# Attention slots in another order: score products, exponentials, transposes and products with v regrouped, projection further ahead

## The chip, the cores and the metric

One core of one Trainium2 chip runs the whole program in one launch. The metric is the device time of one execution, in microseconds (us). An engine here is one of five in-order instruction streams: PE (TensorE, matmuls and transposes), DVE (VectorE), ACT (ScalarE), POOL (GpSimd) and SP (SyncE, which issues most of the DMA transfers).

## The reference, cut to what matters

The program is a trunk of two layers on a sequence of 1024 positions with 1024 features. The first layer mixes positions by a gated MLP; the second by attention; each is followed by a squared-ReLU MLP with 4096 hidden features, and a layer norm closes every part. The change touches the attention of the second layer alone:

```python
def dilated_branch(q, k, v, window, dilation, slopes):
    # blocks of span = window // dilation = 128 positions, each with the block before it
    s = jnp.einsum('bnqrhe,bnkrhe->bnrhqk', qb, kb) * (E ** -0.5)
    s = jnp.where(valid, s + bias, NEG)
    m = jnp.max(s, axis=-1, keepdims=True)
    p = jnp.exp(s - m)
    l = jnp.sum(p, axis=-1, keepdims=True)
    o = jnp.einsum('bnrhqk,bnkrhe->bnqrhe', p / l, vb)
    return o, m + jnp.log(l)

def mixer_b(h, w_qkv, w_out, slopes):
    qkv = (h @ w_qkv).reshape(B, S, 3, 3, 16, 64)
    # three patterns (window, dilation): (128, 1), (512, 4), (2048, 16)
    # each through dilated_branch; the outputs are merged by a softmax over their lse
    return o.reshape(B, S, 1024) @ w_out
```

All of it is float32. A product of two float32 matrices is made of three matmuls: each operand is split into a high part and a low part (`hi`, `lo`), and hi*hi, hi*lo and lo*hi are summed.

## The kernel before

The work of attention is cut by pairs of heads (`hp`, eight of them) and by patterns (`g`, in the order 2, 1, 0; pattern 0 is dilation 1). That makes 24 units, and `attend(n, ...)` (L1367) plans one of them. Each of the 24 units owns eight slots, from `base = 8 * n` on, and reaches over into the slots of the units behind it. A slot has two halves. `at(slot, pos)` (L1362) appends a function to the list of a half slot; at the end (L1774 and following) the halves are gone through in order, the functions of each are called in the order in which they were appended, and behind each half some steps of the projection follow. One step of the projection (`project`, L1323) is three matmuls of 512 columns that add to a sum of q or k (`psq`, `psk`). Steps are dealt out by a credit: 48 of them (`lead = 6 * KD`) come ahead of the first slot, and each half slot earns 464/351 of a step. So PE alternates between small work of the slots and steps of the projection, which fill the time in which the slots wait for ACT and DVE.

The functions of one unit are these:

- `scores(m)` (L1411), for each group of two to four tiles of 128 queries, at the first half of a slot in `starts`: the matmuls `sc` for both heads into two PSUM banks, then for each tile and head a reduction on DVE (L1445: scale, bias, minimum, into `p` and `stat`) and an exponential on ACT (L1447, with a sum). A group has four to eight such pairs.
- `transposes(m)` (L1473), at the second half of a slot: two to four transposes of `p` on PE into a bank `pT`, then the split of that bank: the high part `pThi` on ACT (L102) and the low part `pTlo` on DVE (L103).
- `weighted(m)` (L1486), three half slots later: the products `pv` of `pThi` and `pTlo` with v, into two banks for each head. With the last pack of a head the banks are copied and added into `oT` (L1508 on ACT, L1509 on DVE).
- `merge(hp, ...)` (L1539) joins the three patterns of a pair of heads: statistics go through DRAM (`st_dram`, `mst`), the factors come back as `bc`, and twelve half products (`scale` L1593, `add` L1597, `cut`) on DVE follow, from 16 half slots behind its base on.

The projection splits a sum into `qhi`/`qlo` or `khi`/`klo` (L102, L103), which the scores of patterns 2 and 1 read. Its weights are loaded and split by `unit` (`wq_hi`, `wq_lo`, `wk_hi`, `wk_lo`); the load and the split of a weight are both asked for one unit ahead of its use. Pattern 0 has its q and k from DRAM (`bq`, `bk`).

Toward the end, the output projection begins while attention still runs (`begin`, L1744, matmuls `psoa`, `psob`), with weights that `staged_unit` (L1672) loads, multiplies by a gate (L1682) and splits (`wo_hi`, `wo_lo`). The scheduler that builds the program keeps most of the order in which functions are called, and moves instructions where it takes their inputs to be late.

PSUM banks in attention: two each for `sc`, `pv`, `pT` (kind `tr`) and the projection (kind `mm`).

## Time and profile before

| | us |
|---|---|
| median of three runs | 2759.44 (2755.86 to 2762.37) |
| profiled execution, its own time | 2759.17 |
| its span, first to last instruction | 2757.5 |
| first projection matmul of attention | 1378.7 |
| first score matmul | 1411.6 |
| last reduction of attention | 2042.6 |

The span is shorter than the execution's own time by what lies around the program. In rows of the profile, a line such as L1447 is the place in the kernel's text, a name such as `pv<-pThi,v` tells what is written and what is read, and a bracket behind a row tells how long the engine was idle ahead of it and what it waited for. A row of a stretch has: the stretch, its length, the busy time of PE, PEld (weight loads of PE), DVE, ACT and POOL with counts, the granted share of PE's clock, the share of the DMA engines, and GB/s.

### The profile page before, as it was taken

The numbers are of one execution on the slowest core, as the hardware profiler recorded it, in microseconds if no ns is written. First come the engines' busy times: TensorE is split into PE (matmuls) and PEld (weight loads), VectorE is DVE, ScalarE is ACT, GpSimd is POOL, SyncE is SP. The second block draws the span as 40 slices with busy tenths as digits, with TensorE's granted clock in tenths as the row PEclk, the third lists the DMA queues.
The fourth block names the chain that finished last, engine by engine and source line by source line (L and its number), as shares of the span: only waits on it lengthen the run. The fifth ranks groups of instructions, "written<-read, shape, count | busy, mean of one in ns | idle before, by whom it ended". The sixth has DMA issues, their size and how long they took to land. (4 is left out here: it accounts for less than half of the span.)

```text
span 2757.5 us, 36894 instructions
## 1 busy us (share of the span) xinstructions
PE 2678.4 (97%) x13242; PEld 2206.1 (80%) x13242; DVE 1991.9 (72%) x3594; ACT 1375.1 (50%) x2593; POOL 96.3 (3%) x161
## 2 busy tenths in 40 slices
PE   6999999999999999999999999999999999999998
PEld 5788888887888878888887887778777788878886
DVE  6787698787877788555556676666668966568877
ACT  3354475555443464343445665555564755544432
POOL 1000000000000001111110000000010000000000
PEclk9999999999999999999999999999999999999999
DMA  7534347667836546555556455444573554485562
GB/s 260 161 120 133 115 142 230 217 222 262 317 130 198 177 152 216 194 201 195 182 176 176 120 140 141 110 120 136 169 197 122 185 204 142 153 305 195 175 205 86
DMA packets 332572, 487.98 MB, mean 177 GB/s; under 512 B 50988, under 2 KB 176340, under 8 KB 332388
## 3 DMA queue, kind: packets, MB, share of 16 engines
q1 hardware_dynamic: 318564, 435.29, 49.8%
q0 software_dynamic: 13824, 50.34, 5.1%
q8 instruction: 104, 1.70, 0.3%
q14 instruction: 80, 0.66, 0.1%
HBM read 357.01 MB, written 128.53 MB: 176 GB/s over the span
## 5 line engine op out<-in xcount | busy, mean ns | idle before, releaser
L796 PE MATMUL psua<-right,left 128*128 128x512 f32 x1536 | 364.8, 391 | 0.3
L955 PE MATMUL psd<-rhi,lhi 128*128 128x512 f32 x896 | 350.4, 391 | 3.0 <-ACT part L827 3.0
L955 PE MATMUL psd<-rlo,lhi 128*128 128x512 f32 x896 | 350.3, 391 | 0.2
L955 PE MATMUL psd<-rhi,llo 128*128 128x512 f32 x896 | 349.8, 390 | 0.0
L796 PEld LDWEIGHTS psua<-right,left 128*128 128x128 f32 x1536 | 288.2, 189 | 62.1 <-DVE right L103 1.3
L1447 ACT ACTIVATE p<-p,stat 128x128 f32<-128x128 f32 (+1 forms) x384 | 168.1, 439 | 112.0 <-DVE stat L1445 112.0
L955 PEld LDWEIGHTS psd<-rhi,lhi 128*128 128x128 f32 x896 | 169.1, 189 | 39.3 <-ACT part L827 3.9
L955 PEld LDWEIGHTS psd<-rhi,llo 128*128 128x128 f32 x896 | 169.1, 189 | 35.4
L955 PEld LDWEIGHTS psd<-rlo,lhi 128*128 128x128 f32 x896 | 168.8, 188 | 35.6 <-DVE rlo L103 1.1
L796 PE MATMUL psuc<-right,left 128*128 128x512 f32 x768 | 187.2, 390 | 0.0
L103 DVE TENSOR_TENSOR pTlo<-pT,pThi 128x512 fp32r<-128x512 f32 (+1 forms) x160 | 99.1, 621 | 110.3 <-ACT pThi L102 109.8
L796 PEld LDWEIGHTS psuc<-right,left 128*128 128x128 f32 x768 | 143.5, 188 | 30.0 <-DVE right L103 0.4
L128 DVE SCALAR_TENSOR_TENSOR adaacc<-adaw,silu_c,adaacc 128x512 f32<-128x512 f32 x168 | 128.4, 774 | 54.0 <-DMA adaw<-in_ada_w_dram 53.5
L103 DVE TENSOR_TENSOR left<-ws,left 128x512 fp32r<-128x512 f32 x128 | 87.7, 687 | 72.0 <-ACT left L102 70.2
L103 DVE TENSOR_TENSOR llo<-lraw,lhi 128x1024 fp32r<-128x1024 f32 x112 | 136.3, 1217 | 0.8 <-ACT lhi L102 0.8
L1345 PE MATMUL psq<-form_L,wq_hi 128*128 128x512 f32 x384 | 130.7, 422 | 0.0
L1345 PE MATMUL psk<-form_L,wk_hi 128*128 128x512 f32 x384 | 130.3, 418 | 0.0
L102 ACT CAST left<-ws 128x512 fp32r<-128x512 f32 x128 | 79.1, 620 | 100.3 <-DVE ws L717 87.6
L1257 PE MATMUL psv<-vrhi,form_S 128*128 128x512 f32 x384 | 119.8, 390 | 1.2 <-DVE vpart L1223 0.7
L102 ACT CAST rhi<-rraw 128x1024 fp32r<-128x1024 f32 x48 | 50.6, 1053 | 139.6 <-issue 113.8
L102 ACT CAST lhi<-lraw 128x1024 fp32r<-128x1024 f32 x112 | 117.4, 1048 | 3.4 <-PE psua L796 2.9
L1445 DVE CUSTOM_DVE_ANT_0 p<-sc,bias 128x128 f32<-128x128 f32 (+1 forms) x384 | 110.0, 345 | 7.6 <-PE sc L1431 5.1
(326 smaller groups left out, 6117.7 us busy)
## 6 DMA issues: line engine op xcount, KB each, us to landing
lraw<-forms SPq DMA_DIRECT2D x112, 512.0 KB
adaw<-in_ada_w_dram SPq DMA_DIRECT2D x192, 256.0 KB
up<-in_mlp_w_up_dram SPq DMA_DIRECT2D x64, 512.0 KB
forms<-s SPq DMA_DIRECT2D x128, 256.0 KB
rraw<-in_mlp_w_down_dram SPq DMA_DIRECT2D x64, 512.0 KB
forms<-part SPq DMA_DIRECT2D x96, 256.0 KB
v<-vs POOLq DMA_DIRECT2D x48, 512.0 KB, 3.7
vraw<-in_b_w_qkv_dram SPq DMA_DIRECT2D x42, 512.0 KB
```

Of the source, the lines that this page charges most:

```text
L102: first = A.copy(hi, src) if hi_engine is A else hi_engine.tensor_copy(hi, src)
L103: return first, lo_engine.tensor_tensor(lo, src, hi, op=ALU.subtract)
L128: ins = V.scalar_tensor_tensor(acc[:], raw[:], silu_c[:, k : k + 1], acc[:], ALU.mult, ALU.add)
L796: T.matmul(acc, w[:, a, k, :], right[p][:, b, k, :], start=p in (1, 2, 5) and k + a + b == 0, stop=k == 3 and a == 1, skip_group_check=True)
L955: ins = T.matmul(sums[kind, m][:], l[a][:, k, m * P : (m + 1) * P], r[b][:, k, :], start=p in (1, 5, 2, 3) and kp + k + a + b == 0, stop=k ...
L1257: T.matmul(acc, rows[:, m * P : (m + 1) * P], cols_, start=p in (1, 2, 5) and kp + k + a + b == 0, stop=kp == 1 and k == 1 and a == 1, ski ...
L1345: T.matmul(p[:], wu[a][:, k * P : (k + 1) * P], h_op(k, half, b), start=k + c_ == 0, stop=k == KD - 1 and c_ == 2)
L1445: V.tensor_tensor_reduce(out=pr, in0=banks[e][:, sl], in1=st["bias"][:, width - w :], scale=-0.125, scalar=3e38, op0=ALU.add, op1=ALU.min, ...
L1447: A.activation(pr, pr, AF.Exp, bias=nm, scale=-1.0, accum_out=l)
```

## The change

Each function now goes into its half slot with a rank, and the functions of a half slot are called by rank: transposes and products with v first (0), then score matmuls (1), then the split of the transposed probabilities and the copies out of the `pv` banks (2), then reductions and exponentials (3), then all else (4). The reductions and exponentials of a group leave `scores` and become `soften(m, part)`: the first half of the tiles in the half slot of the scores, the rest in the next half slot. The transposes stand one half slot earlier, and with them the products with v, still three half slots behind. The copies out of the banks (`gather`) come one half slot behind the last product. The merge's twelve pieces start one slot later. The projection's lead is 56 steps instead of 48, and 456/351 of a step follows each half slot. A weight of the projection is loaded three units ahead and split one unit ahead.

```diff
@@ project
-                units = {key: load(*key) for key in todo[:2]}
+                raw, units = {}, {}
+                def load(i):
+                    if i < len(todo):
...
+                        t = raw[i] = wts.tile([P, D], F32, name=f"w{'qk'[X]}_{hp}_{g}_raw", tag="raw", bufs=2)
+                        nc.sync.dma_start(...)
+                def cut(i):
+                    if i < len(todo):
+                        units[todo[i]] = tuple(wts.tile([P, D], F32R, name=f"wqk_{i}_{m}", tag=f"w{m}")[:] for m in ("hi", "lo"))
+                        split(*units[todo[i]], raw.pop(i)[:])
+                for i in range(2):
+                    load(i)
+                cut(0)
+                load(2)
...
                     if half == 1:
-                        if 1 <= i < len(todo) - 1:
-                            units[todo[i + 1]] = load(*todo[i + 1])
+                        cut(i + 1)
+                        load(i + 3)
@@ at
-            def at(slot, pos):
+            def at(slot, pos, rank=4):
                 def put(f):
-                    slots[slot][pos].append(f)
+                    slots[slot][pos].append((rank, f))
                 return put
+            def in_half(half_slot, rank):
+                return at(half_slot // 2, half_slot % 2, rank)
@@ attend
-                    for t, w, sl in spans:
+                    my["spans", m] = banks, spans
+                def soften(m, part):
+                    stat = my["stat"]
+                    banks, spans = my["spans", m]
+                    cut = (len(spans) + 1) // 2
+                    for t, w, sl in spans[cut:] if part else spans[:cut]:
...
-                    at(base + slot, 0)(lambda m=m: scores(m))
+                    at(base + slot, 0, 1)(lambda m=m: scores(m))
+                    for part in range(2):
+                        at(base + slot, part, 3)(lambda m=m, part=part: soften(m, part))
...
+                        pT[m] = pst, end
+                    def halve(m, h=h, pT=pT):
+                        pst, end = pT[m]
                         hi = work.tile([P, HALF], F32R, name=f"pThi_{h}_{g}_{m}", tag="h")
...
-                        if m < len(packs) - 1:
-                            return
+                    def gather(e=e, rows=rows, pvs=pvs):
                         oT = oT_of(e)
...
-                            half_slot = 2 * (base + 5 + 4 * e + w) + 1
+                            half_slot = 2 * (base + 5 + 4 * e + w)
                             then = half_slot + 3
-                        at(half_slot // 2, half_slot % 2)(lambda m=m, f=transposes: f(m))
-                        at(then // 2, then % 2)(lambda m=m, f=weighted: f(m))
+                        in_half(half_slot, 0)(lambda m=m, f=transposes: f(m))
+                        in_half(half_slot, 2)(lambda m=m, f=halve: f(m))
+                        in_half(then, 0)(lambda m=m, f=weighted: f(m))
+                    in_half(then + (not last_one), 2)(gather)
@@ merge
-                    n = pace * n + 16
+                    n = pace * n + 18
@@ the loop over the slots
-            lead, credit = 6 * KD, 0
+            lead, credit = 7 * KD, 0
...
-                    for f in pos:
+                    for _, f in sorted(pos, key=lambda x_: x_[0]):
                         f()
```

What this makes of the order shows at three places. The first is ACT in the fourth pair of heads, where the second group of pattern 2 (`p_6_2`, `p_7_2`) has its exponentials, while the pair before still transposes (`pThi_5_0_3` is the high part of head 5, pattern 0, pack 3). Before:

```order
L1447 ACTIVATE p_6_2_4_14420,stat_3_2_14209<-p_6_2_4_14420,stat_3_2_14209 128x128
L1447 ACTIVATE p_7_2_4_14423,stat_3_2_14209<-p_7_2_4_14423,stat_3_2_14209 128x128
L1447 ACTIVATE p_6_2_4_14420,stat_3_2_14209<-p_6_2_4_14420,stat_3_2_14209 128x128
L1447 ACTIVATE p_7_2_4_14423,stat_3_2_14209<-p_7_2_4_14423,stat_3_2_14209 128x128
L1447 ACTIVATE p_6_2_6_14430,stat_3_2_14209<-p_6_2_6_14430,stat_3_2_14209 128x128
L1447 ACTIVATE p_7_2_6_14433,stat_3_2_14209<-p_7_2_6_14433,stat_3_2_14209 128x128
L1447 ACTIVATE p_6_2_6_14430,stat_3_2_14209<-p_6_2_6_14430,stat_3_2_14209 128x128
L1447 ACTIVATE p_7_2_6_14433,stat_3_2_14209<-p_7_2_6_14433,stat_3_2_14209 128x128
L102 COPY pThi_5_0_3_14451<-pT_5_0_3_14447 128x384
```

On the same engine at the same place now:

```order
L102 COPY pThi_5_0_3_14425<-pT_5_0_3_14395 128x384
L1469 ACTIVATE p_6_2_4_14429,stat_3_2_14243<-p_6_2_4_14429,stat_3_2_14243 128x128
L1469 ACTIVATE p_7_2_4_14432,stat_3_2_14243<-p_7_2_4_14432,stat_3_2_14243 128x128
L1469 ACTIVATE p_6_2_4_14429,stat_3_2_14243<-p_6_2_4_14429,stat_3_2_14243 128x128
L1469 ACTIVATE p_7_2_4_14432,stat_3_2_14243<-p_7_2_4_14432,stat_3_2_14243 128x128
L1469 ACTIVATE p_6_2_6_14465,stat_3_2_14243<-p_6_2_6_14465,stat_3_2_14243 128x128
```

The high part has moved from behind the eight exponentials to ahead of them. The second place is DVE a little later, ahead of the first group of pattern 1 (`p_6_1_0`), whose scores read `klo_3_1`. Before:

```order
L103 TENSOR_TENSOR pTlo_6_2_0_14497<-pT_6_2_0_14491,pThi_6_2_0_14496 128x512
L1593 TENSOR_TENSOR bc_2_2_14458<-oT_2_2_13674,bc_2_2_14458 128x512
L103 TENSOR_TENSOR wk_4_1_lo_14981<-wk_4_1_raw_14978,wk_4_1_hi_14980 128x1024
L103 TENSOR_TENSOR klo_3_1_14283<-psk_3_1_0_14440,khi_3_1_14282 128x4x128
L1509 TENSOR_TENSOR oT_3_2_14616<-oT_3_2_14616,pv_6_2_0_14524 64x512
L1445 ISA p_6_1_0_14559,stat_3_1_14534<-sc_6_1_0_14539,bias_6_1_14535 128x128
```

DVE at the same place now:

```order
L103 TENSOR_TENSOR klo_3_1_14222<-psk_3_1_0_14358,khi_3_1_14221 128x4x128
L103 TENSOR_TENSOR wqk_19_lo_14927<-wk_4_1_raw_14496,wqk_19_hi_14926 128x1024
L1537 TENSOR_TENSOR oT_2_0_14349<-oT_2_0_14349,pv_5_0_1_14363 64x512
L103 TENSOR_TENSOR pTlo_6_2_0_14521<-pT_6_2_0_14511,pThi_6_2_0_14520 128x512
L1537 TENSOR_TENSOR oT_3_2_14653<-oT_3_2_14653,pv_6_2_0_14536 64x512
L103 TENSOR_TENSOR pTlo_6_2_1_14580<-pT_6_2_1_14549,pThi_6_2_1_14579 128x512
L1467 ISA p_6_1_0_14583,stat_3_1_14554<-sc_6_1_0_14559,bias_6_1_14555 128x128
```

The low part of k has moved ahead of the weight's low part, and the merge's product (`bc_2_2`) has left this place. The third place is DVE in the last pair of heads, where the weights of the output projection are prepared (`wo_0` to `wo_3`) and the merge of the pair before runs (`bc_6`). Before, these rows stood ahead of the reductions of the first group of pattern 1 (`p_14_1_0`), with the low parts of `wo_0` and `wo_1` a few rows ahead of them:

```order
L1682 TENSOR_TENSOR wo_2_raw_18254<-wo_2_raw_18254,gate_2_18126 128x1024
L1682 TENSOR_TENSOR wo_3_raw_18291<-wo_3_raw_18291,gate_2_18126 128x1024
L103 TENSOR_TENSOR wo_2_lo_18297<-wo_2_raw_18254,wo_2_hi_18296 128x1024
L1593 TENSOR_TENSOR bc_6_2_18236<-oT_6_2_17449,bc_6_2_18236 128x512
L1445 ISA p_14_1_0_18353,stat_7_1_18328<-sc_14_1_0_18333,bias_14_1_18329 128x128
```

DVE there now, from the reductions of the next group (`p_15_1_3`) on:

```order
L1467 ISA p_15_1_3_18457,stat_7_1_18332<-sc_15_1_1_18432,bias_15_1_18335 128x256
L1467 ISA stat_7_1_18332 128x1
L1712 TENSOR_TENSOR wo_2_raw_18254<-wo_2_raw_18254,gate_2_18135 128x1024
L103 TENSOR_TENSOR wo_1_lo_18288<-wo_1_raw_18137,wo_1_hi_18287 128x1024
L1623 TENSOR_TENSOR bc_6_1_18237<-oT_6_1_17766,bc_6_1_18237 128x512
L103 TENSOR_TENSOR wo_2_lo_18297<-wo_2_raw_18254,wo_2_hi_18296 128x1024
L1467 ISA p_14_1_5_18461,stat_7_1_18332<-sc_14_1_1_18431,bias_14_1_18333 128x256
```

The low parts of `wo_1` and `wo_2` have moved from ahead of the reductions of the first group of pattern 1 into those of the second.

8 lines of the change are left out of this document (4 added, 4 removed).

## The prediction

> **What bounds the kernel now.** I read the page's busy times first, then the busy times of two stretches, then who waited for whom in the first of them, and last the instructions in order of time around two of those waits.
>
> ```profile
> span 2757.5 us, 36894 instructions
> PE 2678.4 (97%) x13242; PEld 2206.1 (80%) x13242; DVE 1991.9 (72%) x3594; ACT 1375.1 (50%) x2593; POOL 96.3 (3%) x161
> 1412.00:1978.00 566.00, 547.86 (x3570) 454.39 (x3568) 379.06 (x1154) 334.99 (x1010) 20.57 (x48) 0.98 0.49 132
> 1978.00:2080.00 102.00, 94.02 (x553) 76.71 (x551) 74.68 (x184) 56.87 (x146) 10.07 (x12) 0.95 0.76 200
> ```
>
> PE is busy for 97% of the span, so only PE's idle time, the overlap it loses around a wait, and its clock can be won. The change touches attention alone. Its even part runs from 1412 to 1978 us: there PE is idle for 566.0 - 547.9 = 18.1 us and has 0.98 of its clock, while DVE (379 of 566) and ACT (335 of 566) have room. Everything ahead of 1412 and behind 2080 us stays as it is, bound by PE.
>
> The waits of PE, and then those of its weight loads, in that stretch (total, times, longest):
>
> ```profile
> PE pv L1499 <- ACT pThi L102: 8.9, 12, 1.7
> PE sc L1431 <- DVE klo L103: 6.1, 4, 2.1
> PE pv L1499 <- DVE pTlo L103: 2.0, 8, 0.4
> PEld pv L1499 <- ACT pThi L102: 16.8, 18, 2.1
> PEld pv L1499 <- DVE pTlo L103: 9.3, 25, 0.5
> PEld sc L1431 <- DVE klo L103: 6.7, 4, 2.2
> ```
>
> Two things are late. One is the high and low part of the transposed probabilities, which the products with v (pv) need. This is one such place:
>
> ```profile
> 1657.03 0.27 PE L1476 MATMUL pT<-ident,p 128*128 128x128 f32 x1
> 1657.95 0.40 ACT L1447 ACTIVATE p<-p,stat 128x128 f32<-128x128 f32 x1 [1.69 <-DVE stat L1445]
> 1659.01 0.62 PE L1345 MATMUL psk<-form_L,wk_hi 128*128 128x512 f32 x2
> 1659.70 0.62 PE L1345 MATMUL psk<-form_L,wk_hi 128*128 128x512 f32 x2
> 1661.05 0.46 ACT L102 CAST pThi<-pT 128x384 fp32r<-128x384 f32 x1
> 1661.56 0.38 PE L1499 MATMUL pv<-pThi,v 128*128 128x256 f32 x1 [1.00 <-ACT pThi L102]
> 1662.15 0.38 PE L1499 MATMUL pv<-pTlo,v 128*128 128x256 f32 x1 [0.21 <-DVE pTlo L103]
> ```
>
> The last transpose is done at 1657.3. Its high part starts only at 1661.05, since ACT runs the eight exponentials of a group first, from 1657.95 on. PE reaches the products at about 1660.6 and stands.
>
> The other late thing is the low part of k, without which the scores of the next group cannot go on:
>
> ```profile
> 1666.79 1.05 DVE L1593 TENSOR_TENSOR bc<-oT,bc 128x512 f32<-128x512 f32 x1 [1.50 <-DMA bc<-w_dram]
> 1667.77 1.21 DVE L103 TENSOR_TENSOR wk_lo<-wk_raw,wk_hi 128x1024 fp32r<-128x1024 f32 x1
> 1668.90 0.68 DVE L103 TENSOR_TENSOR klo<-psk,khi 128x512 fp32r<-128x512 f32 x1
> 1669.63 0.33 PE L1431 MATMUL sc<-klo,qhi 64*128 64x128 f32 x2 [1.86 <-DVE klo L103]
> ```
>
> DVE first waits 1.50 us for a transfer that a merge needs, then does the merge's product and a weight's low part, and klo last. PE pays 1.86 us. Four stretches around such waits show what follows (the third column from the end is the granted clock):
>
> ```profile
> 1666.00:1676.00 10.00, 8.14 (x48) 6.84 (x48) 6.00 (x18) 3.80 (x14) 0.00 (x0) 0.83 0.71 189
> 1741.00:1751.00 10.00, 8.29 (x37) 6.30 (x35) 4.94 (x10) 5.31 (x18) 0.81 (x2) 0.83 0.87 215
> 1830.00:1840.00 10.00, 7.96 (x48) 6.54 (x46) 6.75 (x19) 3.80 (x14) 0.00 (x0) 0.83 0.71 183
> 1909.00:1921.00 12.00, 9.94 (x50) 8.30 (x49) 6.71 (x19) 5.19 (x16) 0.00 (x0) 0.72 0.62 167
> ```
>
> PE works slower for some us after each.
>
> **The change, part by part.** Nothing is computed more or less often: the rows on each engine are the same in kind and number, only their places move. So every price is a wait that goes or comes.
>
> *Parts ahead of exponentials (ranks, two halves, transposes half a slot earlier).* On ACT the high part now stands ahead of the group's exponentials, and at most the second half of the group before, four exponentials, stands ahead of it. From the transposes to their products it is still three half slots. The loss today: PE idle 8.9 + 2.0 = 10.9 us, and each of the 18 + 25 = 43 waits of a load also loses the overlap of two matmuls. Three projection matmuls take 1659.70 - 1659.01 = 0.69 us, so one starts each 0.23 us, while a pair shows 0.62 and thus a single one 0.39: 0.16 us lost per wait, 43 x 0.16 = 6.9 us. Together 17.8 us. I take 15.3 of it, since a weight's high part (1.05 us on ACT) or a copy still gets between now and then; the bounds are 9 and 17.8.
>
> *k in time (eight more projection steps ahead, the merge a slot later, ranks).* The lead grows from 48 to 56 steps, that is 8 x 0.69 = 5.5 us of PE work moved ahead of the first scores. It costs nothing, as the same work is missing later: 464/351 steps per half slot become 456/351, and both streams end at half slot 351. At the wait shown (slot 80 of 175) about 4 of the 8 steps of lead are left, and on DVE klo now stands ahead of the weight's part and the merge's product. A stall of 2 us is covered by either. PE's 6.1 us are worth 4 x 0.16 more: 6.7, and I take 6.2, bounds 5 and 6.7; the last pairs keep little of the lead.
>
> *The clock.* The four stretches lose 3 x 10 x 0.17 + 12 x 0.28 = 8.5 us. Each follows directly on an idle time of PE of 1.7 to 2.1 us. With those waits gone I count all of it back: 8.5, bounds 0 and 8.5. Yet of two equal waits the second brought a drop and the first did not:
>
> ```profile
> 1516.18 0.33 PE L1499 MATMUL pv<-pThi,v 128*128 128x128 f32 x1 [1.69 <-ACT pThi L102]
> 1743.45 0.39 PE L1499 MATMUL pv<-pThi,v 128*128 128x256 f32 x1 [1.71 <-ACT pThi L102]
> 1514.00:1524.00 10.00, 8.08 (x48) 6.12 (x46) 6.29 (x17) 5.85 (x20) 0.00 (x0) 1.00 0.15 43
> ```
>
> So the link is not one to one. [...]
>
> *Products and the copies out of them (gather) later.* The copies of a head's sums come half a slot later than its last product. The next head's first product needs the first bank only, and the order still has that bank's copy ahead of the head's last parts. Price zero; without that cover each of the 48 heads would wait for a copy and an addition:
>
> ```profile
> L102 ACT CAST wq_hi<-wq_raw 128x1024 fp32r<-128x1024 f32 x13 | 13.7, 1055 | 5.2 <-PE psq L1345 5.1
> L1447 ACT ACTIVATE p<-p,stat 128x128 f32<-128x128 f32 (+1 forms) x344 | 150.2, 438 | 103.6 <-DVE stat L1445 103.5
> L1508 ACT COPY oT<-pv 64x512 f32<-64x512 f32 x82 | 47.6, 581 | 60.4 <-PE pv L1499 59.3
> L103 DVE TENSOR_TENSOR pTlo<-pT,pThi 128x512 fp32r<-128x512 f32 (+1 forms) x138 | 85.5, 621 | 95.8 <-ACT pThi L102 95.4
> L1509 DVE TENSOR_TENSOR oT<-oT,pv 64x512 f32<-64x512 f32 x82 | 56.0, 683 | 24.2 <-ACT oT L1508 22.7
> L1593 DVE TENSOR_TENSOR bc<-oT,bc 128x512 f32<-128x512 f32 x36 | 33.0, 934 | 7.9 <-DMA bc<-w_dram 7.8
> L1445 DVE CUSTOM_DVE_ANT_0 p<-sc,bias 128x128 f32<-128x128 f32 (+1 forms) x344 | 98.0, 343 | 7.3 <-PE sc L1431 4.9 <-issue 1.8
> ```
>
> *Weights loaded two units earlier.* On SP a load now waits until the weight in its buffer has been split, about 2.3 us (1.05 on ACT, 1.22 on DVE). Behind it stand loads of v and of q and k blocks and the merge's small ones, all asked for a slot or more ahead (the first and the third of the four stretches lie 164 us, or two pairs of heads of 24 slots, apart: a slot is 3.4 us). Price zero, and up to 3 us if one of them had no such lead.
>
> *The merge a slot later.* DVE's 7.8 us of waiting for bc go. The four oT buffers come free a slot later, and the next one is asked for eight slots on. Zero.
>
> *The end of attention.* This speaks against the change. From 1985 on PE fills its time with the output projection (psoa), whose weights DVE prepares:
>
> ```profile
> 2004.43 1.22 DVE L103 TENSOR_TENSOR wo_lo<-wo_raw,wo_hi 128x1024 fp32r<-128x1024 f32 x1
> 1986.73 0.39 PE L1499 MATMUL pv<-pThi,v 128*128 128x256 f32 x1 [0.54 <-ACT pThi L102]
> 2005.71 0.50 PE L1726 MATMUL psoa<-wo_lo,oTs 128*128 128x512 f32 x1 [0.18 <-DVE wo_lo L103]
> 1931.45 1.16 PE sc L1431 x18
> 1934.54 0.84 PE pv L1499 x8
> ```
>
> Before, between the reductions of that group (p_14_1_0) and the end of wo_3's low part DVE has six reductions, a pTlo, three merge products and the part itself: 6 x 0.343 + 0.62 + 3 x 0.93 + 1.22 = 6.7 us. Now it has ten reductions, six merge products, two copies' additions, two pTlo, a merge addition (as long as klo's 0.68) and five weight operations ahead of that point: 3.4 + 5.6 + 1.4 + 1.2 + 0.7 + 6.1 = 18.4 us. PE has some 11 us of its own until there (48 score rows at 1.16/18, 31 transposes and products at 0.84/8, 20 psoa at 0.23: 3.1 + 3.3 + 4.6). So it stands for about 8 us, where the eight waits of before between 1985 and 2007, whose first and last are shown, sum to 3.4: 5 us more, and 1 us for the clock. I take +6, bounds 0 and +12 (the whole 11.7 us of delay).
>
> **Sum**, against the profiled execution's own time of 2759.17 us (span 2757.5 and 1.7 around it; the median of the runs is 2759.44, 0.3 away): 15.3 + 6.2 + 8.5 = 30.0 won, 6 lost, so 2759.2 - 24.0 = 2735.2. **I predict 2735 us.**
>
> **Rivals.**
> [...]
> - *The parts stay late.* ACT's high parts still come behind a second half of exponentials, 4 x (0.44 + a readout) on ACT and a weight's part; then half of 17.8 comes back and part of the clock is not won: 2735 + 6.4 + 6 = 2747 to 2753. Against: three half slots are 5.1 us, and ACT is busy for 335 of 566.
> - *The end takes it back.* DVE becomes the bound there (74.7 busy of 102 us already), the delay of 11.7 us falls on PE in full, and the clock is halved twice as long: 12 + 3.4 + a late chain of transfers behind it, 2745 to 2759.
> - *Slower: the banks of the products.* Each head's sums are copied half a slot later. If the copy of the first bank comes behind the next head's parts, PE stands at 48 changes of head for a copy and an addition, 0.58 + 0.68 = 1.27 us, 61 us in all; with 24 won, 2796. It decides from the point where the first bank's copy starts less than 1.3 us ahead of the next head's first product; half of the heads at that price already give 2765. For it: the copies stand behind the parts now. Against: the order keeps the first bank's copy two packs ahead.
> - That the scheduler sorts the rows back is ruled out by the rows in the section on the change.
>
> **How the numbers follow.** Chances: forecast 0.56, clock stays 0.10, parts late 0.12, end takes it back 0.10, banks 0.12. The low end is all three gains at their upper bounds and a tail that costs nothing, 2759 - 33 = 2726, less some 6 us of waits in the tail (3.4 and clock) that might go too: 2720. The high end is the lower bounds, 9 + 5 + 0, against a loss of 12: 2757. The range 2720 to 2757 takes in all but the banks, and a little of the end's case. A measurement of this kernel can tell about 0.2%, 5.5 us, from no change. Faster by more: 0.56 + 0.10 + 0.09 + 0.04 = 0.79. Within: 0.03 + 0.05 = 0.08. Slower: 0.01 + 0.12 = 0.13.
>
> **What would show it.** In the changed profile, in the stretch that answers to 1412 to 1978: PE's waits for pThi and pTlo fall from 10.9 us to about 2, those for klo from 6.1 to under 1, the granted clock is 1.00, and the stretch is some 30 us shorter. In the end, PE waits more for wo parts and pTlo, DVE in front of it. Waits of pv for DVE's or ACT's oT would mean the banks. The prediction is wrong if pT begins to wait for the exponentials, since transposes come half a slot earlier and second halves half a slot later, or if the stretch is free of waits and yet no shorter.

## The result and the profile after

| | before | changed |
|---|---|---|
| median of the runs, us | 2760.03 (2755.86 to 2762.37, 4 runs) | 2727.61 (2725.15 to 2728.55, 4 runs) |
| profiled execution, its own time | 2759.17 | 2727.96 |
| first to last projection matmul | 611.9 (1378.9 to 1990.7) | 579.4 (1377.0 to 1956.4) |
| from there to the last psoa or psoe | 134.8 (to 2125.6) | 139.0 (to 2095.4) |

The change made the kernel faster: the ratio is 0.9883, 95% interval 0.9866 to 0.9900. In the profiled executions 31.2 us went. The stretch of the projection gave 32.5, the end of attention took 4.2 back, and 3.0 came from outside attention (1.9 ahead, 1.1 behind). Those 3.0 are probably not the change's: before has stretches at half clock (granted share 0.50) of 3.41 us each at 424 and 2441 us that this profile lacks, and another execution with the changed order (no_lead, below) has one at 423 us again.

In the code after, the lines that matter have moved: L1345 is L1358 (projection), L1431 is L1447 (`sc`), L1445 and L1447 are L1467 and L1469 (reductions, exponentials), L1499 is L1527 (`pv`), L1508 and L1509 are L1536 and L1537 (copies into `oT`), L1593 is L1623 (the merge's product `bc`), L1726 is L1756 (`psoa`).

The page of the changed kernel, span and busy times:

```profile
span 2726.2 us, 36911 instructions
PE 2658.8 (98%) x13242; PEld 2196.3 (81%) x13242; DVE 1989.8 (73%) x3594; ACT 1377.1 (51%) x2593; POOL 97.0 (4%) x161
```

The number of instructions on each of these engines is as before. PE's busy time fell from 2678.4 to 2658.8 us with the same instructions: the profile shows matmuls at half clock, and those right behind a wait, as longer (a projection matmul in before 0.63 us at 1672.2, at half clock, and 0.39 us at 1673.9, at full clock again; a `pv` of 128x128 in the changed kernel 0.33 us at 1967.7, behind a wait, and 0.27 to 0.28 us from 1968.7 to 1969.1). Now the projection's stretch and the end of attention, first of before, then of the changed kernel (stretch, length, busy times of PE, PEld, DVE, ACT and POOL, granted clock, DMA share, GB/s):

```profile
1379.00:1991.00 612.00, 593.12 (x3795) 491.46 (x3793) 405.44 (x1209) 352.59 (x1047) 26.23 (x57) 0.99 0.51 141
1991.00:2126.00 135.00, 125.91 (x681) 102.48 (x680) 101.93 (x245) 72.50 (x160) 8.21 (x10) 0.96 0.62 173
```

```profile
1377.00:1957.00 580.00, 576.82 (x3798) 483.94 (x3798) 402.68 (x1208) 353.63 (x1047) 27.09 (x57) 1.00 0.54 149
1957.00:2096.00 139.00, 127.87 (x679) 104.24 (x678) 102.86 (x246) 73.63 (x160) 7.70 (x10) 0.95 0.62 167
```

PE's idle time in the stretch went from 18.9 to 3.2 us, and its clock is whole. DVE and ACT do the same work in less time. PE's waits there in the changed kernel, all that the trace has (total, times, longest):

```profile
PE pv L1527 <- DVE pTlo L103: 2.7, 4, 1.2
PE pv L1527 <- ACT pThi L102: 0.3, 1, 0.3
```

Waits for `klo` are gone, waits for the parts fell from 10.9 us to 3.0. This is the place of the first `order` pair of the change, a pack of three transposes beside the exponentials of the second group:

```profile
1649.52 0.27 PE L1500 MATMUL pT<-ident,p 128*128 128x128 f32 x1
1649.83 0.48 ACT L102 CAST pThi<-pT 128x384 fp32r<-128x384 f32 x1 [0.60 <-PE pT L1500]
1651.65 0.40 ACT L1469 ACTIVATE p<-p,stat 128x128 f32<-128x128 f32 x1 [1.34 <-DVE stat L1467]
...
1654.58 0.29 PE L1527 MATMUL pv<-pThi,v 128*128 128x256 f32 x1
```

The high part starts as soon as the last transpose is done (1649.52 + 0.27; in before 3.75 us behind it), ahead of the exponentials. PE reaches the products 4.3 us later and does not stand. One number went the wrong way, DVE's wait for the merge's factors (the group of all products of the merge, with the idle time ahead of them):

```profile
L1623 DVE TENSOR_TENSOR bc<-oT,bc 128x512 f32<-128x512 f32 x48 | 45.0, 944 | 19.8 <-DMA bc<-w_dram 16.2 <-issue 3.6
```

Before it was 7.8 us, all for `bc`; of the 19.8 us now, 16.2 are for `bc`, and for 3.6 the trace names nothing that was waited for. Most of the experiments turn on it. And in the end of attention, these rows stand around PE's longest wait:

```profile
1963.92 1.98 DVE L1623 TENSOR_TENSOR bc<-oT,bc 128x512 f32<-128x512 f32 x2 [1.97 <-DMA bc<-w_dram]
1965.99 1.07 ACT L1536 COPY oT<-pv 64x512 f32<-64x512 f32 x2 [2.69 <-DVE bc L1623]
1967.08 0.58 ACT L102 CAST pThi<-pT 128x512 fp32r<-128x512 f32 x1
1967.71 0.33 PE L1527 MATMUL pv<-pThi,v 128*128 128x128 f32 x1 [3.26 <-ACT pThi L102]
```

Read from the top: DVE stands for `bc`; the copy out of `pv` needs a buffer of `oT` that this product still reads, so ACT stands; the high part is queued behind the copy; PE stands. No weight of the output projection is in this chain. PE's second longest wait there is another matter:

```profile
1976.36 1.21 DVE L1712 TENSOR_TENSOR wo_raw<-wo_raw,gate 128x1024 f32<-128x1024 f32 x1
1977.50 0.67 DVE L103 TENSOR_TENSOR pTlo<-pT,pThi 128x512 fp32r<-128x512 f32 x1
1978.22 0.33 PE L1527 MATMUL pv<-pTlo,v 128*128 128x128 f32 x1 [2.27 <-DVE pTlo L103]
```

The high part of this pack was done by 1972.5, but DVE had work without a pause from 1966.6 on. From 1969.09 to the low part that is four operations on weights of the output projection (4.8 us), four merge products (3.3 us) and two reductions. This is the queue that the prediction had described.

### The profile page after: what moved, and what is told of

The parts are those of the page before. It is cut to its first block, busy times and chain, and to the rows that moved or that the text cites. A ratio compares the mean times of both kernels' runs of the same rounds, so it can differ in the third digit from the quotient of the medians.

```text
span 2726.2 us, 36911 instructions
## 1 busy us (share of the span) xinstructions
PE 2658.8 (98%) x13242; PEld 2196.3 (81%) x13242; DVE 1989.8 (73%) x3594; ACT 1377.1 (51%) x2593; POOL 97.0 (4%) x161
## 4 chain that ended last, share of the span: by engine, by line
PE 77%; DVE 12%; DMA 6%; ACT 3%; issue 2%; SPq 1%; DVEq 0%; ACTq 0%
PE psd L955 22%; PE psv L1257 13%; PE psua L796 7%; PE psq L1358 6%; PE psk L1358 6%; DMA adaw<-in_ada_w_dram 3%; PE psuc L796 3%; PE psd_wout L389 3%; PE psu L368 3%; PE pv L1527 3%; PE sc L1447 2%; PE psv L470 2%; PE psub L796 2%; DVE adaacc L128 1%; DVE left L103 1%
## 5 line engine op out<-in xcount | busy, mean ns | idle before, releaser
L1469 ACT ACTIVATE p<-p,stat 128x128 f32<-128x128 f32 (+1 forms) x384 | 168.7, 441 | 107.8 <-DVE stat L1467 104.7
L1358 PE MATMUL psk<-form_L,wqk_hi 128*128 128x512 f32 x384 | 127.0, 412 | 0.0
L1358 PE MATMUL psq<-form_L,wqk_hi 128*128 128x512 f32 x384 | 126.4, 410 | 0.0
L1467 DVE CUSTOM_DVE_ANT_0 p<-sc,bias 128x128 f32<-128x128 f32 (+1 forms) x384 | 113.6, 346 | 6.7 <-PE sc L1447 5.8
```

The lines of the kernel that those rows point to most:

```text
L1358: T.matmul(p[:], wu[a][:, k * P : (k + 1) * P], h_op(k, half, b), start=k + c_ == 0, stop=k == KD - 1 and c_ == 2)
L1467: V.tensor_tensor_reduce(out=pr, in0=banks[e][:, sl], in1=st["bias"][:, width - w :], scale=-0.125, scalar=3e38, op0=ALU.add, op1=ALU.min, ...
L1469: A.activation(pr, pr, AF.Exp, bias=nm, scale=-1.0, accum_out=l)
```

## The experiments

Twelve kernels. The theory held at first was that of the prediction: the parts were late because exponentials stood ahead of them on ACT, k because the lead was short and DVE's order bad, and the clock followed PE's waits. "Stretch" is from the first to the last projection matmul and "end" from there to the last psoa or psoe, both of the profiled execution; "bc" is DVE's idle time ahead of the merge's products from 1377 to 1990 us. It is time spent waiting for `bc`, but for 3.6 us in changed and in merge_16 and all 6.1 us in old_factors, for which the trace names nothing that was waited for. Each ratio is to executions of the kernel before made beside that kernel, whose median lay between 2756.9 and 2760.0 us. Medians of different experiments can therefore differ by some 3 us for no cause in the kernel.

| kernel | median us | ratio to before, 95% interval | stretch | end | bc |
|---|---|---|---|---|---|
| before | 2760.03 | | 611.9 | 134.8 | 7.8 |
| changed | 2727.61 | 0.9883, 0.9866 to 0.9900 | 579.4 | 139.0 | 19.8 |
| lead_only | 2759.23 | 1.0002, 0.9993 to 1.0010 | 614.9 | 135.4 | 11.7 |
| no_lead | 2727.11 | 0.9888, 0.9871 to 0.9905 | 575.2 | 138.9 | 18.4 |
| no_halves | 2734.17 | 0.9912, 0.9898 to 0.9926 | 583.6 | 141.7 | 20.1 |
| odd_transposes | 2748.76 | 0.9964, 0.9950 to 0.9977 | 603.2 | 136.6 | 19.2 |
| old_place | 2745.24 | 0.9951, 0.9938 to 0.9964 | 596.8 | 138.7 | 9.4 |
| old_merge_20 | 2743.90 | 0.9949, 0.9933 to 0.9965 | 594.7 | 137.3 | 7.4 |
| merge_20 | 2729.26 | 0.9896, 0.9879 to 0.9912 | 576.9 | 140.0 | 4.5 |
| merge_16 | 2733.48 | 0.9910, 0.9894 to 0.9927 | 586.2 | 139.4 | 22.9 |
| first_factors | 2755.48 | 0.9986, 0.9972 to 1.0001 | 605.8 | 136.8 | 16.5 |
| old_factors | 2736.40 | 0.9918, 0.9898 to 0.9938 | 589.8 | 138.4 | 6.1 |
| factors | 2722.89 | 0.9870, 0.9849 to 0.9892 | 577.6 | 135.0 | 3.3 |
| factors_wo | 2724.69 | 0.9866, 0.9842 to 0.9889 | 579.8 | 133.5 | 3.0 |

### The lead: lead_only and no_lead

In the kernel before (lead_only):

```diff
-            lead, credit = 6 * KD, 0
+            lead, credit = 7 * KD, 0
```

> The kernel before, with nothing changed but the projection's lead (56 steps for 48). Theory (the waits for klo come from too short a lead, those for the high parts from the exponentials ahead of them on ACT, and the clock falls behind any wait of some 1.7 us): PE's waits for klo go from 6.1 us to under 1, those of pv for pThi and pTlo stay at about 11 us, and of the four half-clock stretches between 1660 and 1920 us three go (the one at 1742 us follows a wait for pThi): 6.2 + 6.8 = 13 us won, about 2747 us. Rival (klo is late because of what stands ahead of it on DVE, the merge's product and the weight's part, not because of the lead): at most 3 us won, 2756 us or more, and the drops of the clock stay.

Measured: no difference. PE's waits in the stretch, 1378 to 1993 us:

```profile
PE pv L1499 <- ACT pThi L102: 11.8, 12, 3.1
PE pv L1499 <- DVE pTlo L103: 6.5, 13, 3.1
PE sc L1431 <- DVE klo L103: 3.1, 1, 3.1
```

Of the three long waits for `klo` in before (1.9 to 2.1 us) two went, as the theory said, and the third grew to 3.1. Two new waits of 3.1 us for the parts came at other places, and the time at half clock is 20.5 us where before has 17.1. One of the new waits, at 1509.3, is for a high part behind eight exponentials. The other, for a low part at 1592.8, stands behind this row:

```profile
1590.64 1.03 DVE L1593 TENSOR_TENSOR bc<-oT,bc 128x512 f32<-128x512 f32 x1 [4.92 <-DMA bc<-w_dram]
```

So the waits that PE lost by more lead were made up for by others, one of them behind the merge's transfer. That each new wait is an old one moved on is not shown.

And the other way in the changed kernel (no_lead):

```diff
-            lead, credit = 7 * KD, 0
+            lead, credit = 6 * KD, 0
```

> The changed kernel, with 48 steps of the projection ahead instead of 56. Theory (k is in time by its place on DVE, and the longer lead only adds to that): 0 to 4 us slower than 2727.6, with at most one wait for klo above 1 us. Rival (the lead is what brings k in time): three or four waits for klo of about 2 us and their drops come back, 6 + 7 = 13 us: 2741 us.

Measured: 2727.11, the theory's case. Its only wait in the stretch, 1380 to 1955 us:

```profile
PE sc L1447 <- DVE klo L103: 0.5, 1, 0.5
```

So the lead is worth nothing that shows, alone or beside the rest. Of the reasons given for `klo`, its place in DVE's queue is left; it was not tried alone.

### The places of transposes and exponentials: no_halves, odd_transposes, old_place

All in the changed kernel. First, no_halves:

```diff
-                        at(base + slot, part, 3)(lambda m=m, part=part: soften(m, part))
+                        at(base + slot, 0, 3)(lambda m=m, part=part: soften(m, part))
```

> The changed kernel, with all reductions and exponentials of a group in the half slot of its scores; the high part of the pack transposed there still stands ahead of them. Theory (what counts is that the parts of the same half slot come first): 0 to 3 us slower than the changed kernel's 2727.6, since only the next pack's part, one half slot on, has eight exponentials ahead of it rather than four, and it has three half slots of time. Rival (the halves carry the gain of the parts): about 10 us slower, 2738 us, with waits of pv for pThi of 5 us or more back in the stretch of the projection.

Measured: 6.6 us by the medians, between the two. Waits of pv did not come back; other waits did:

```profile
1514.55 1.08 DVE L1623 TENSOR_TENSOR bc<-oT,bc 128x512 f32<-128x512 f32 x1 [3.76 <-DMA bc<-w_dram]
1515.55 0.29 DVE L1467 CUSTOM_DVE_ANT_0 p<-sc,bias 128x128 f32<-128x128 f32 x1
...
1517.01 0.59 PE L1447 MATMUL sc<-khi,qhi 64*128 64x256 f32 x2 [1.45 <-DVE stat L1467]
```

DVE stands 3.76 us for `bc` with the whole group's reductions behind it, and the scores wait for the banks that those reductions still read. Here, as in one wait of lead_only, the merge's transfer stood at the root.

Then odd_transposes:

```diff
-                            half_slot = 2 * (base + 5 + 4 * e + w)
+                            half_slot = 2 * (base + 5 + 4 * e + w) + 1
```

> The changed kernel, with transposes and products with v one half slot later again, where the kernel before had them. Of the packs that meet a group's exponentials, the high part has four of them ahead of it instead of none. Theory (each 0.44 us exponential ahead of the part on ACT delays it, and four are 1.8 us against the 3.3 us and more of eight): 2 to 6 us slower than 2727.6. Rival 1 (the earlier place of the transposes is the whole gain): 15 us slower, 2743. Rival 2 (the place does not matter, the lead of k and the ranks do it all): within 2 us.

Measured: 21.2 us slower than the changed kernel, more than the larger rival gave. The longest of PE's waits, and the granted clock around it:

```profile
1518.29 1.02 DVE L1623 TENSOR_TENSOR bc<-oT,bc 128x512 f32<-128x512 f32 x1 [4.95 <-DMA bc<-w_dram]
1519.22 0.68 DVE L103 TENSOR_TENSOR pTlo<-pT,pThi 128x512 fp32r<-128x512 f32 x1
...
1519.96 0.48 PE L1527 MATMUL pv<-pTlo,v 128*128 128x128 f32 x1 [4.23 <-DVE pTlo L103]
```

```profile
1510.00:1530.00 20.00, 15.77 (x94) 13.29 (x94) 11.68 (x31) 9.17 (x27) 0.00 (x0) 0.83 0.61 151
```

The high part of that pack was done at 1514.5; its low part stood behind the merge's product, which waited. In the changed kernel the pack is transposed half a slot sooner, and its low part is made ahead of the group's reductions and of the product, which waits there too (1516.0, 3.52 us):

```profile
1509.93 0.69 DVE L103 TENSOR_TENSOR pTlo<-pT,pThi 128x512 fp32r<-128x512 f32 x1 [1.25 <-ACT pThi L102]
```

Both edits together (old_place) put the high part behind all eight exponentials, as in the kernel before, and leave lead, loads, merge and ranks as changed.

> The changed kernel, with the transposes one half slot later again and all exponentials of a group in the half slot of its scores: the high part that meets a group stands behind its eight exponentials, as in the kernel before, while lead, loads, merge and klo stay as changed. Theory (the eight exponentials make the waits of pv): PE's waits for pThi and pTlo in the stretch of the projection go back to 9 to 11 us, with 4 to 7 us in the loads beside them, waits for klo stay under 1 us: 13 to 17 us slower than 2727.6 by the waits, and by 2 to 7 us more if the half-clock stretches come back behind waits of pv alone: 2741 to 2751. Rival (the waits of pv came from elsewhere, from the merge or a weight's part on ACT): under 6 us slower, 2733 or less.

Measured: 17.6 us slower than the changed kernel, in the middle of the theory's range, and 14.8 us faster than before. But the longest wait has another cause than the theory's:

```profile
1592.92 1.03 DVE L1623 TENSOR_TENSOR bc<-oT,bc 128x512 f32<-128x512 f32 x1 [3.94 <-DMA bc<-w_dram]
1593.87 0.28 DVE L1467 CUSTOM_DVE_ANT_0 p<-sc,bias 128x128 f32<-128x128 f32 x1
...
1596.85 0.59 ACT L102 CAST pThi<-pT 128x512 fp32r<-128x512 f32 x1
...
1597.48 0.47 PE L1527 MATMUL pv<-pThi,v 128*128 128x128 f32 x1 [4.59 <-ACT pThi L102]
```

The exponentials ahead of the part wait for reductions, and those for `bc`. The number fitted; the reason did not. A new theory: in these kernels DVE's wait for `bc` makes the long waits of PE, and the exponentials only the short ones.

### The merge's pieces: old_merge_20, merge_20, merge_16

On old_place (old_merge_20) and on the changed kernel (merge_20):

```diff
-                    n = pace * n + 18
+                    n = pace * n + 20
```

> As old_place (transposes one half slot later, all eight exponentials together), and the merge's twelve pieces one slot later still. In old_place PE's two longest waits in the stretch (4.59 us for pThi at 1597.5, 2.27 us for pTlo at 1678.7) each follow a merge product for which DVE stood 3.94 and 3.39 us, waiting for bc, with the group's reductions or the pTlo queued behind it. Theory (DVE's wait for bc makes the waits of pv, and exponentials ahead of the part cost little): both go, and the drops of the clock behind them (10.2 + 3.4 us at half clock, 6.8 us): 6.9 + 6.8 = 13 us won, 2732 us, and DVE's waits for bc fall from 9.4 us to under 2. Rival (the eight exponentials ahead of the high part are enough to make PE wait): within 4 us of old_place's 2745.

Measured: 1.3 us. This run does not decide, since its edit missed its aim: DVE still waits 7.4 us, and the product still stands ahead of a low part.

```profile
1595.27 1.96 DVE L1623 TENSOR_TENSOR bc<-oT,bc 128x512 f32<-128x512 f32 x2 [4.36 <-DMA bc<-w_dram]
1597.15 0.68 DVE L103 TENSOR_TENSOR pTlo<-pT,pThi 128x512 fp32r<-128x512 f32 x1
...
1597.89 0.48 PE L1527 MATMUL pv<-pTlo,v 128*128 128x128 f32 x1 [4.04 <-DVE pTlo L103]
```

> The changed kernel, with the merge's pieces one slot later still. There DVE waits 16.2 us for bc, and of PE's waits in the stretch the two longest (0.77 us at 1520.1, 1.16 us at 1595.5, both for pTlo) follow such a wait. Theory: DVE's waits for bc fall to under 3 us, PE wins those two waits and what they cost in overlap, 2 to 3 us: 2725 us, if the end, into which the last merges move, loses nothing. Rival (the later merge of the pair before last lands in the end, where DVE is busy 74 of 139 us): 3 to 6 us slower, 2731 to 2734.

Measured: no gain by the medians (2729.26). In the profile, which is of the fastest of its five executions, the stretch is 2.5 us shorter, as expected, and the end 1.0 us longer, with a wait of 3.55 us that was not there:

```profile
1964.98 0.80 PE L1756 MATMUL psoa<-wo_lo,oTs 128*128 128x512 f32 x1 [3.55 <-DVE wo_lo L103]
```

And on the changed kernel the other way (merge_16):

```diff
-                    n = pace * n + 18
+                    n = pace * n + 16
```

> The changed kernel, with the merge's pieces where they were before the change. Theory (DVE's wait for bc is what the later merge spares): DVE waits up to a slot, 3.4 us, longer for bc in each of the pairs, work that PE needs stands behind it, PE gets two to five waits of 1.5 to 4 us with drops of the clock behind those of 1.8 us and more: 8 to 15 us slower than 2727.6, 2736 to 2743. Rival (nothing that PE needs soon stands behind the product, since ranks put it last in its half slot): within 2 us.

Measured: 5.9 us slower, below the theory's 8 to 15 and clear of the rival's 2. Two waits of PE of 1.8 to 2.1 us came, each with a drop of the clock; one of them:

```profile
1597.49 2.02 DVE L1623 TENSOR_TENSOR bc<-oT,bc 128x512 f32<-128x512 f32 x2 [1.24 <-DMA bc<-w_dram]
1599.42 0.67 DVE L1537 TENSOR_TENSOR oT<-oT,pv 64x512 f32<-64x512 f32 x1
1600.02 0.68 DVE L103 TENSOR_TENSOR pTlo<-pT,pThi 128x512 fp32r<-128x512 f32 x1
...
1600.75 0.33 PE L1527 MATMUL pv<-pTlo,v 128*128 128x128 f32 x1 [2.06 <-DVE pTlo L103]
```

So the later merge earns some 6 to 7 us of the change's gain (5.9 by the medians, 7.4 by the ratios). It does so although DVE waits long for `bc` in the changed kernel too: what counts is what stands behind the wait.

### The transfer itself: first_factors, old_factors, factors

Instead of moving the products, these three let `bc` arrive earlier, in the kernel before, in old_place and in the changed kernel: its factors are worked out and spread one slot sooner.

```diff
-                @at(*((base + 4, 0) if hp < N_PAIRS - 1 else (base + 1, 0)))
+                @at(*((base + 3, 0) if hp < N_PAIRS - 1 else (base + 1, 0)))
                 def factors():
...
-                @at(*((base + 4, 1) if hp < N_PAIRS - 1 else (base + 1, 0)))
+                @at(*((base + 3, 1) if hp < N_PAIRS - 1 else (base + 1, 0)))
                 def spread():
```

> The kernel before, with nothing changed but that the merge's factors are worked out and spread (ma, w_dram, bc) one slot earlier. In it DVE waits 7.8 us for bc in six pairs, and three of PE's four waits for klo (1.86, 2.04 and 2.06 us) stand right behind such a wait and the product after it. Theory (klo is late because DVE stands for bc): DVE's waits for bc go, PE's waits for klo fall from 6.1 us to under 2, with the three drops of the clock behind them (3.4 + 3.4 + 6.8 us at half clock): 4 to 6 + up to 6.8 us won, 2747 to 2751 us against 2759.5; the waits for pThi (8.9 us) stay. Rival 1 (only the order of rows on DVE counts): within 2 us. Rival 2 (a wait taken away comes back at the next place, as with the longer lead alone): within 3 us, with more waits of pv than before.

Measured: not to be told from no change (2755.48; the interval takes in 1). The wait for `bc` grew to 16.5 us instead of going. DVE in the third pair of heads:

```profile
1584.33 1.09 DVE L1593 TENSOR_TENSOR bc<-oT,bc 128x512 f32<-128x512 f32 x1 [2.46 <-DMA bc<-w_dram]
...
1587.31 1.22 DVE L103 TENSOR_TENSOR wk_lo<-wk_raw,wk_hi 128x1024 fp32r<-128x1024 f32 x1
1588.56 0.69 DVE L103 TENSOR_TENSOR klo<-psk,khi 128x512 fp32r<-128x512 f32 x1
...
1589.31 0.32 PE L1431 MATMUL sc<-klo,qhi 64*128 64x128 f32 x1 [2.09 <-DVE klo L103]
```

In the kernel before, the first product stood behind `wk_lo` and `klo` here, at 1588.2. The scheduler, which now took `bc` to be early, moved the product ahead of both, where the transfer was still under way. So this does not say what `klo` would do if `bc` were in time. It says that an earlier transfer is worth nothing to a queue that uses it at once.

> As old_place (transposes a half slot later, eight exponentials together), with the merge's factors one slot earlier. Moving the merge's pieces a slot later left DVE's wait for bc where it was (7.4 us in two places), with a pTlo behind it. Theory (bc makes the long waits of pv in old_place): DVE's waits for bc fall from 9.4 to under 2 us, the two long waits (4.59 and 2.27 us) and their drops go, 6.9 + 6.8 us: about 2732 us. Rival (the exponentials ahead of the part make PE wait): within 4 us of old_place's 2745.

Measured: 8.8 us faster than old_place, two thirds of what the new theory gave. PE's waits in the stretch, 1378 to 1968 us:

```profile
PE pv L1527 <- DVE pTlo L103: 5.6, 8, 2.7
PE pv L1527 <- ACT pThi L102: 1.3, 2, 0.9
```

The waits of 4.59 and 2.27 us are gone; of the drops one of 3.4 us is left (13.7 us in old_place). Some 9 us of old_place's loss hung on when `bc` arrives. The rest is not all of the other theory. DVE still stands 3.3 and 2.8 us ahead of two merge products. The trace names nothing that it waited for, but each product starts 4.8 to 4.9 us after the first load of its `bc` was issued, and in factors, where the wait is put down to `bc`, it is 5.0:

```profile
1583.87 1.98 DVE L1623 TENSOR_TENSOR bc<-oT,bc 128x512 f32<-128x512 f32 x2 [3.32 <-issue]
```

PE's two longest waits, 2.71 us at 1587.0 with the one drop and 1.30 us at 1663.9, are for low parts behind these two products.

> The changed kernel, with the merge's factors one slot earlier. Theory: DVE's waits for bc fall from 16.2 us to under 4. In the stretch of the projection that is worth the 1.9 us of the two waits for pTlo that follow them, and their overlap; in the end it takes away the wait of 3.26 us at 1967.7 (there the product stands 1.97 us for bc, the copy out of pv on ACT stands 2.69 us until that product has let go of oT, and pThi stands behind the copy) and the drop at 1969, 1.7 us: 5 to 7 us faster than 2727.6, 2721 to 2723. Rival (the weights of the output projection fill DVE there, and pThi or a wo part is late anyway): within 2 us.

Measured: 2722.89, 4.7 us below the changed kernel by the medians, within what was expected, and 3.6 us by the ratios. Its runs (2719.29 to 2725.49) hardly overlap those of the changed kernel, the intervals of the ratios do, so the sign is likely and the size not settled. The wait for `bc` is down to one, the end as long as in the kernel before:

```profile
DVE bc L1623 <- DMA bc<-w_dram: 3.3, 1, 3.3
```

```profile
1956.00:2091.00 135.00, 125.38 (x680) 101.69 (x680) 102.53 (x245) 72.86 (x159) 8.21 (x10) 0.97 0.63 175
```

The waits of 3.26 us at 1967.7 and of 2.27 us at 1978.2 are gone, with the weights of the output projection where the changed kernel has them. And factors against old_factors is the nearest to a clean comparison of the places: the same kernel but for the transposes and the halves, 13.5 us apart. Of this some 3 us are still the merge's, by my estimate: old_factors has the two waits (2.71 and 1.30 us) and the drop (1.7 us) told above, factors one wait of 2.35 us behind a merge product and no drop.

### The weights of the end: factors_wo

On factors:

```diff
-            @at(last_group - 13, 0)
+            @at(last_group - 17, 0)
...
-            staged_unit(0, (-14, 0), (-12, 0), (-11, 0))
-            staged_unit(1, (-13, 0), (-11, 1), (-10, 1))
-            staged_unit(2, (-11, 0), (-10, 0), (-9, 0))
+            staged_unit(0, (-17, 0), (-15, 0), (-14, 0))
+            staged_unit(1, (-16, 0), (-14, 1), (-13, 1))
+            staged_unit(2, (-14, 0), (-13, 0), (-12, 0))
```

> As factors (the merge's factors one slot earlier), with the first three weights of the output projection loaded, multiplied and split three slots earlier, and the gate's row four. In factors the end is 135.0 us long, as in the kernel before (134.8). PE still waits there 1.95 us at 1962.4 for oTs to be loaded, 0.44 us for a wo_lo and 1.02 us for a wo_hi. Theory of the prediction (the weights' work on DVE and ACT makes the end late): the two waits for weights and some of the drop at 1962.9 go, 1.5 to 3 us faster than factors' 2722.9. Rival (bc was the whole loss of the end, and weights staged earlier only meet the last pairs' parts on DVE and ACT): between no gain and 4 us slower, 2723 to 2727.

Measured: 2724.69, the rival's case by the medians; by the ratios it is 1.1 us faster than factors, and the intervals lie almost over each other. No difference can be told. The profile is of the slowest of its four executions (2727.86). PE's waits in the end, of factors (1956 to 2091) and of factors_wo (1960 to 2093):

```profile
PE pv L1527 <- DVE pTlo L103: 2.8, 4, 0.9
PE psoa L1756 <- DMA oTs<-o_dram: 1.9, 1, 1.9
...
PE psoa L1756 <- ACT wo_hi L102: 1.0, 1, 1.0
```

```profile
PE pv L1527 <- DVE pTlo L103: 2.1, 4, 0.9
PE pv L1527 <- ACT pThi L102: 2.1, 2, 1.7
```

The waits for weights went, and a wait for `pThi` of 1.7 us came. The profiled end is 1.5 us shorter, the stretch 2.2 us longer, with one drop of the clock. So with `bc` in time, moving the weights' work wins nothing that can be measured.

## Why the prediction was right, and where its steps were not

The time was 7.4 us below the forecast, inside the range. For the sizes I summed how much later each of PE's instructions starts after the one before it than is usual for that pair of kinds (the 20th percentile of the pair; delays over 0.13 us, those in stretches at half clock apart).

- *Parts ahead of exponentials, 15.3.* Late starts of pv: 19.5 us in before, 4.7 in the changed kernel, so 14.9 won. The size was right, the reason only in part. Factors against old_factors gives 13.5 us for the places, of which some 3 are the merge's; but with the places as before, another 9 us (old_place against old_factors) hang on when `bc` arrives. The step did not have that link, so some luck is in the size.
- *k in time, 6.2.* Late starts of the score matmuls that read `klo`: 14.7 to 8.5 us, 6.1 won, as much as PE's waits for `klo` (6.1 us before, none now); the 8.5 that are left follow no such wait. Of the reasons given, "eight more projection steps ahead" failed: no_lead has the whole gain without them, and lead_only has them and no gain. The place of `klo` on DVE, given beside it, is what is left; three of the four waits for it in the kernel before followed a wait for `bc`. It was not tried alone.
- *The clock, 8.5.* All of it: the 17.1 us at half clock in before's stretch are gone. Half of them is 8.5; the late starts give 9.2. The link that was called "not one to one" is indeed not: in the changed kernel a drop of 6.83 us follows a wait of 0.95 us, in before none follows one of 1.69 us. Yet of the 43 idle times of 1.8 us or longer in the fourteen traces 42 have a drop (last section).
- *Sum of the stretch, 30.0.* 14.9 + 6.1 + 9.2 = 30.2 by the late starts, 32.5 measured.
- *The merge a slot later, "DVE's 7.8 us of waiting for bc go. ... Zero."* This step failed. The waits for `bc` grew to 16.2 us (19.8 with the idle time that the trace puts down to nothing), and they are not free: one of them makes the end's longest wait, and factors, which takes most of them away, is 4.7 us faster by the medians (the sign is likely, the size not settled). The four `oT` buffers, also priced at zero, are the link in that chain.
- *The end of attention, +6.* +4.2 measured, only in part by the way that the step named. It had DVE's 18.4 us of work, the weights above all, ahead of wo_3's low part. PE's longest wait (3.26 us) came instead from `bc` over the `oT` buffer and the copy to `pThi`. The second longest (2.27 us) did stand behind weights and merge products on DVE, at a `pTlo`. But factors leaves the weights where they are, has neither wait, and its end is 135.0, and factors_wo moves the weights and wins no time that can be told. So that the size came near is partly luck.
- *Products and copies later, and the banks as the rival.* No wait of pv for `oT` or a bank is among PE's waits in the changed kernel's stretch. Zero was right.
- *Loads two units earlier, zero.* No wait of PE points to them; they were not tried alone.
- *The 7.2 us between the forecast and the profiled execution* are 2.5 in the stretch, 1.8 in the end and 3.0 outside attention, probably stretches at half clock, which no step dealt with.

What stays open: why odd_transposes, with halves, is slower than old_place without them; and why the merge's transfer comes later against DVE's work in the changed kernel: around the third pair its six loads are issued from 1582.6 on, where before has 1580.5, though attention is ahead by then.

## What to carry to other kernels

Before moving a late instruction, look at what stands ahead of it in its engine's queue and what *that* waits for: here a transfer of the merge, off the path by every total, decided much of how long PE stood, by what happened to be queued behind it. More lead alone took waits from the bound engine and others came, for no gain; ordering the helpers' queues by who needs the result first kept them away. And a total that fits is no proof of its reason: old_place landed in the middle of the expected range, and its longest wait began with a transfer that the theory did not have.

## What the runs showed of the hardware

In the stretches called half clock the granted share is 0.50. In the fourteen profiled executions, from 1380 to 2140 us, PE was idle 43 times for 1.8 us or longer, and 42 times a stretch at half clock began within 3.5 us of the end of that wait or during it. Of ten idle times of 1.4 to 1.8 us six had one, of 46 from 0.9 to 1.4 us twelve. The one long wait without a drop is of 2.35 us, in factors (to 1585.1). These are all the stretches at half clock in that part of the traces of before and of the changed kernel, with the longest idle time of PE that ended in the 3.5 us ahead of the start or lay across it:

| kernel | start, us | length, us | idle time of PE, us | its end, us |
|---|---|---|---|---|
| before | 1670.06 | 3.41 | 1.86 | 1669.63 |
| before | 1745.15 | 3.41 | 1.71 | 1743.45 |
| before | 1833.89 | 3.41 | 2.04 | 1833.14 |
| before | 1912.40 | 6.83 | 2.06 | 1912.89 |
| before | 1994.32 | 3.41 | 0.48 | 1993.25 |
| before | 2059.17 | 6.83 | 2.43 | 2057.53 |
| changed | 1969.29 | 3.41 | 3.26 | 1967.71 |
| changed | 1979.53 | 3.41 | 2.27 | 1978.22 |
| changed | 2030.73 | 6.83 | 0.95 | 2030.47 |

No stretch at half clock follows the idle times of 1.69, 0.91, 1.00 and 1.18 us in before (to 1516.2, 1582.5, 1661.6 and 2103.3) or those of 1.16 and 1.18 us in the changed kernel (to 1595.5 and 2073.2). So the two equal waits of the prediction, 1.69 us without a drop and 1.71 us with one, lie at lengths at which the fourteen traces have both. In the clock record of the whole trace of the changed kernel, the starts at 679.0, 1969.3, 1979.5 and 2030.7 us lie 186, 564, 567 and 582 times 3.413 us behind the first, at 44.2 us. What decides whether a wait brings a drop, and why some drops last 6.83 us, was not shown: no kernel was made to try it.
